# Reordering a decoder layer: the state space branch's input projection ahead of the third attention group, and gate z ahead of the third gate

## The chip, the cores and the metric

The kernel runs on one core of a Trainium2 chip. The metric is the device time of one execution in microseconds (us), the median of three runs. The profile is of one execution more, recorded by the hardware profiler. TensorE (PE in the profile, PEld for its weight loads) multiplies matrices into PSUM; VectorE (DVE), ScalarE (ACT) and GpSimd (POOL) work elementwise; SyncE (SP) issues the DMA transfers.

## The reference

One decoder layer on a sequence of 512 positions of width 1024, all in fp32. A normalised input `u` is projected once, the projection is cut into pieces, and three branches are formed from them, gated and added:

```python
u = rmsnorm(x, ln1_g[i])
proj = u @ w_in[i]
q, k, v, pool_in, z, xbc, dt_raw, gate_pre = jnp.split(proj, split_idx, axis=-1)
y_a = dilated_attention_mixer(q, k, v, rel_bias) @ w_a[i]
y_b = pool_mixer(pool_in, pool_w[i], pool_scale[i]) @ w_b[i]
y_c = ssd_mixer(z, xbc, dt_raw, ...) @ w_c[i]
gates = jax.nn.sigmoid(gate_pre + b_gate[i]).reshape(b, s, N_BRANCH, D_MODEL)
merged = gates[:, :, 0] * y_a + gates[:, :, 1] * y_b + gates[:, :, 2] * y_c
x = x + merged @ w_o[i]
x = x + conv_ffn(rmsnorm(x, ln2_g[i]), ...)
```

- `dilated_attention_mixer`: three groups of six heads (dilations 1, 4, 16), each with its own softmax; their outputs are combined per head by a softmax over the groups' log-sum-exps.
- `ssd_mixer`: a causal convolution of four taps and a Silu on `xbc` (1536 columns: 1024 for x, 256 each for B and C), then a state space scan in four chunks of 128 positions and two groups of eight heads, then a product with `silu(z)`, then a norm over each group's 512 columns.

## The kernel before, in words

**Matmuls.** Every large product is done as three products of split operands (high by high, high by low, low by high; `mm3`, L209). The high part of a weight is a cast on ScalarE (`split`, L176), the low part a subtraction on VectorE (L180).

**Jobs.** The work is a list of `Job`s, one for each weight tile, made by `program()`. Most hold 256 columns of a weight with all 1024 rows (1 MB): two chunks of 128 columns, 24 matmuls of 512 columns each. When job n starts, the main loop's `prepare` splits the weight of job n+1 and fetches those of n+2 and n+3. For n under 34 (`HALVES`) the split is done in two halves, the second at the next step; from 34 on it is done whole, right at the start of the job. `Call` entries between jobs run a function in place.

**Steps and items.** After each chunk (or after two of the four row blocks of a v job, each half of whose 1024 rows is a job) the job calls `step()` (L132). A step advances each generator in the list `running` to its next `yield`, oldest first, then takes the first one from the list `waiting`, starts it and adds it to `running`. So small work is laid between the chunks, and its instructions stand in this order on TensorE, ScalarE, VectorE and GpSimd (`ORDERED`); each of these engines works strictly in that order. SyncE's transfers are ordered by the framework. The items:
- attention (`attend`, `item`): one for each head. For a pair of heads the first item does both score products into two PSUM tiles (L500); each item adds the bias (L514), takes the negative maximum (L518) and does the exponentials with their sums (L521); two steps later it transposes (L527) and copies (L528); the second head of a pair goes on a step later with the product with v (L539). `stats` transposes the maxima and sums (L552, L554).
- `combine`: the weights of the three groups (L570 to L581), a reciprocal (L583), a multiplication on GpSimd (L587), a write to DRAM (L588) and broadcast reads of it into tiles `wb` (L594), with which GpSimd scales the nine output tiles (L596). `split_o` adds and splits them (L602 to L607).
- state space: `xbc_evac` convolves each chunk (L663, L667); `ssd_start` puts the Silus (L827), two transposes and eight `ssd_item`s on the list, with an empty place after each. An `ssd_item` starts with a transpose pxs (L768) and a product pcb (L774), broadcast reads into `al` and `ea`, subtracts and exponentiates (L785, L786), multiplies (L790), and four steps after its start does the products py, pyo and pst (L800, L806, L817), which VectorE adds up (L808, L809, L812, L822).
- `gated` multiplies a chunk by gate z (L853), squares it (L855) and adds the squares (L859): two of the three additions of a group on GpSimd, the last on VectorE. `y_norm` sums over the partitions on TensorE (pss, L867), forms the factor on VectorE and ScalarE (`rstd_of`, L279 to L288, L871), spreads it by TensorE (prb, L875) and scales and splits four tiles (L878 to L885).

**Buffers.** Eight PSUM banks: four tiles tagged "mm" for the chunks, four tagged "sm" for all small products. 52 SBUF tiles of 128x512 (`NBIG`) are shared under one tag.

**The order around the change.** For each attention group: v (two jobs), q and k (three), then `attend` puts its items on the list, so they run beside the next jobs. After the third group come `combine`, the `xbc` projection (six jobs), the first gate (four jobs; the state space items start with its first), then a hand-written row of jobs, `MIX`: g is a job of the third gate, Z and z one of gate z for the first and second half, 0 and 1 put `y_norm` of that half on the list, a is a job of w_a. Before MIX is over what is left on the list is run down by `finish`, then comes w_c.

Of the kernel before, what the change touches and what calls it, by code (L numbers as in the profile page):

```python
# [19 lines left out]
KD = D // P  # L20
# [14 lines left out]
C_XBC = C_Z + D  # L35
# [46 lines left out]
def trunk(ctx: ExitStack, tc, out, x, rel_bias, ln1_g, w_in, b_gate, w_a, pool_w, pool_scale, w_b,  # L82
# [41 lines left out]


    waiting, running = [], []

    second = []

# [4 lines left out]
    def step():  # L134
        flush()
        for it in list(running):
            try:
                next(it)
            except StopIteration:
                running.remove(it)  # L140
        if waiting:
            it = waiting.pop(0)
            running.append(it)
            try:
                next(it)
            except StopIteration:
                running.remove(it)

    def after(n, it):
        for _ in range(n):  # L150
            yield
        yield from it
# [324 lines left out]
    def attend(g):  # L477
        nm = cpool.tile([P, 4, HEADS], F32, name=f"nm{g}")
        ls = cpool.tile([P, 4, HEADS], F32, name=f"ls{g}")
        if g == 0:  # L480
            banks = [[(1, 0, 2), (2, 1, 2)], [(3, 2, 2), (0, 0, 1)]]
        else:
            banks = [[(n, n, 1) for n in range(4)]]
        outs, probs, scores = {}, {}, {}

        def item(h, nb, bank):
            c, hh = h // 2, h % 2
            b = bias_of(g, h)
            off, spans = 0, []
            for n, kb, w in bank:  # L490
                spans.append((n, kb, w, off))
                off += w * P
            if hh == 0:

                q, k = QK["q", g, c], QK["k", g, c]
                pss = [SM("ps"), SM("ps")]
                for n, kb, w, o in spans:
                    for i in range(2):
                        r = slice(DH * i, DH * i + DH)
                        pe.matmul(pss[i][:, o:o + w * P], q[r, n * P:(n + 1) * P],  # L500
                                  k[r, kb * P:(kb + w) * P], start=True, stop=True)
                scores[c, nb] = pss
            ps = scores[c, nb][hh]
            total = off
            sb = T("sb")
            if g == 0 and total == 384:
                dve.tensor_tensor(sb[:, :256], ps[:, :256], b, OP.add)
                dve.tensor_tensor(sb[:, 256:384], ps[:, 256:384], b[:, P:], OP.add)
                for n, kb, w, off in spans:
                    dve.tensor_reduce(nm[:, n, h:h + 1], sb[:, off:off + w * P],  # L510
                                      AX.X, OP.max, negate=True)
            else:
                n = len(bank)
                dve.tensor_tensor(sb.rearrange("p (n c) -> p n c", n=n),  # L514
                                  ps.rearrange("p (n c) -> p n c", n=n),
                                  b.unsqueeze(1).to_broadcast([P, n, S // n]), OP.add)
                n0 = bank[0][0]
                dve.tensor_reduce(nm[:, n0:n0 + n, h], sb.rearrange("p (n c) -> p n c", n=n),  # L518
                                  AX.X, OP.max, negate=True)
            for n, kb, w, off in spans:  # L520
                act.activation(sb[:, off:off + w * P], sb[:, off:off + w * P], AF.Exp,  # L521
                               bias=nm[:, n, h:h + 1], accum_out=ls[:, n, h:h + 1])
            yield
            yield
            pt = SM("pt")
            for o in range(0, total, P):
                pe.transpose(pt[:, o:o + P], sb[:, o:o + P], eye)  # L527
            (act.copy if h % 2 else dve.tensor_copy)(sb[:, :total], pt[:, :total])  # L528
            probs[h, nb] = sb
            if h % 2 == 0:  # L530
                return
            yield
            if c not in outs:
                outs[c] = SM("po")
            po = outs[c]
            for n, kb, w, off in spans:
                for i in range(w):
                    for hh in range(2):
                        pe.matmul(po[DH * hh:DH * hh + DH, n * P:(n + 1) * P],  # L539
                                  V[g, kb + i][:, (2 * c + hh) * DH:(2 * c + hh + 1) * DH],  # L540
                                  probs[2 * c + hh, nb][:, off + i * P:off + (i + 1) * P],
                                  start=i == 0, stop=i == w - 1)
            if nb == len(banks) - 1:
                o = T(f"o{g}")
                act.copy(blocked(o, g), grouped(po, g))
                OT[g, c] = o

        def stats():
            for src, store, nme in ((nm, NM, "nmT"), (ls, LS, "lsT")):
                ps = SM("pst")  # L550
                for n in range(4):
                    pe.transpose(ps[:HEADS, n * P:(n + 1) * P], src[:, n, :], eye)  # L552
                t = T(nme)
                dve.tensor_copy(blocked(t[:HEADS], g), grouped(ps[:HEADS], g))  # L554
                store[g] = t
            return
            yield

        for c in range(3):
            for nb, bank in enumerate(banks):  # L560
                for hh in range(2):
                    waiting.append(item(2 * c + hh, nb, bank))
        waiting.append(after(2, stats()))

    AO = []

    def combine():
        mm, den, tmp = T("mmin"), T("den"), T("dtmp")
        yield
        dve.tensor_tensor(mm[:HEADS], NM[0][:HEADS], NM[1][:HEADS], OP.min)  # L570
        dve.tensor_tensor(mm[:HEADS], mm[:HEADS], NM[2][:HEADS], OP.min)
        for g in range(3):
            n = NM[g][:HEADS]
            dve.tensor_tensor(n, mm[:HEADS], n, OP.subtract)
            act.activation(n, n, AF.Exp)
        yield
        for g in range(3):
            n, l = NM[g][:HEADS], LS[g][:HEADS]
            dve.tensor_tensor(tmp[:HEADS] if g else den[:HEADS], n, l, OP.mult)
            if g:  # L580
                dve.tensor_tensor(den[:HEADS], den[:HEADS], tmp[:HEADS], OP.add)  # L581
        yield
        dve.reciprocal(tmp[:HEADS], den[:HEADS])  # L583
        wd = dram.tile([3, HEADS, S], F32, name="wd")
        for g in range(3):
            n = NM[g][:HEADS]
            pool.tensor_tensor(n, n, tmp[:HEADS], OP.mult)  # L587
            sp.dma_start(wd[g], n)  # L588
        yield
        for c in range(3):  # L590
            for g in range(3):
                wb = T("wb")
                for hh in range(2):
                    sp.dma_start(wb[DH * hh:DH * hh + DH, :],  # L594
                                 wd[g, 2 * c + hh, :].partition_broadcast(DH))
                pool.tensor_tensor(OT[g, c], OT[g, c], wb, OP.mult)  # L596
                if (3 * c + g) % 2:
                    yield

    def split_o(c):  # L600
        for g in (1, 2):
            dve.tensor_tensor(OT[0, c], OT[0, c], OT[g, c], OP.add)  # L602
        ah, al = T("ah", F32R), T("al", F32R)
        act.copy(ah, OT[0, c])
        AO.append((ah, al))
        yield
        dve.tensor_sub(al, OT[0, c], ah.bitcast(F32))  # L607
# [217 lines left out]
    def ssd_start():  # L825
        for m in (8, 9, 0, 1, 2, 3, 10, 4, 5, 6, 7, 11):
            act.activation(XS[m], XS[m], AF.Silu)  # L827
        for gi in range(2):
            waiting.append(btok_item(gi))
        for c, gi, gap in SSD_ORDER:  # L830
            waiting.append(ssd_item(c, gi))
            for _ in range(gap):
                waiting.append(iter(()))
        for c in range(3):
            waiting.append(split_o(c))

    SQ = {0: [], 1: []}

# [250 lines left out]
    def program():  # L1089
# [5 lines left out]
        for g in range(3):  # L1095
# [2 lines left out]
            yield Call(lambda g=g: attend(g))  # L1098
            if g == 0:
                yield Call(lambda: waiting.insert(5, ssd_prep()))  # L1100
        yield Call(lambda: waiting.append(combine()))
        yield from jobs_a(w_in, C_XBC, 12, uhk, ulk, KD, xbc_evac)
        for i, job in enumerate(gate_jobs(0)):
            if i == 0:
                job.body = lambda ws, inner=job.body: (ssd_start(), inner(ws))
            yield job
        many = {"a": branch_jobs(0, w_a, AO, 3), "g": gate_jobs(2),
                "Z": z_jobs(0), "z": z_jobs(1)}
        for token in MIX:
# [185 lines left out]
ORDERED = {EngineType.PE, EngineType.Activation, EngineType.DVE, EngineType.Pool}  # L1295
NBIG = 52
HALVES = 0, 34
MIX = "gggZZ0zzg1aa"
SSD_ORDER = ((0, 0, 1), (1, 0, 1), (0, 1, 1), (2, 0, 1), (1, 1, 1), (3, 0, 1), (2, 1, 1), (3, 1, 1))
WARM = 12  # L1300

# [28 lines left out]
```

## Time and profile before

| | |
|---|---|
| Median of 3 runs | 1066.93 us (1065.83 to 1067.12) |
| Profiled execution | 1067.88 us, of which the span is 1065.7 us |
| Mean granted TensorE clock | 0.994 of full speed |
| DMA | 115.50 MB, mean 108 GB/s |
| GpSimd busy | 13% of the span, in 118 instructions |

The span runs from the first to the last instruction that the profile shows; the rest of the execution's time lies around it. In the profile "L209" is line 209 of the kernel; names such as `pa` or `wl` are tiles; "a<-b,c" is output and inputs; a bracket behind an instruction gives the time for which its engine sat idle before it and what ended that. A line may stand for several instructions in a row (x8).

### The profile page before, as it was taken

What the parts mean: (1) busy time and instruction counts of PE and PEld (TensorE: products, weight loads), DVE (VectorE), ACT (ScalarE), POOL (GpSimd) and SP (SyncE); (2) the same over time, 40 slices, a digit from 0 to 9 for tenths busy, and PEclk for the clock granted to TensorE, in tenths of its full rate; (3) what the DMA queues carried; (4) which work ended last, traced back from release to release, by engine and by line L of the source; (5) the groups of instructions that cost most, each with busy time, mean ns of one, the idle gap of its engine ahead of it and who ended that gap; (6) DMA issues with size and microseconds to landing.
All of it is one profiled execution on the core that took longest, in us unless ns stands there. A gap on an engine that the chain in (4) does not pass through costs nothing.

```text
span 1065.7 us, 12968 instructions
## 1 busy us (share of the span) xinstructions
PE 1047.1 (98%) x5268; PEld 874.1 (82%) x5268; DVE 584.9 (55%) x809; ACT 427.8 (40%) x640; POOL 133.3 (13%) x118
## 2 busy tenths in 40 slices
PE   8999999999999999999999799999999999999997
PEld 8878889888988888877888588898888888888885
DVE  5562433245544668586687856757655565542315
ACT  5342412232435356555544324544444344421312
POOL 1680000000000000621012300001111111110100
PEclk9999999999999999999999899999999999999999
DMA  7235324341542222654322135543232323232312
GB/s 235 77 107 158 109 73 108 98 110 60 143 110 77 81 79 79 178 164 126 90 77 98 54 114 198 163 138 117 83 117 79 117 82 115 83 119 61 117 60 79
DMA packets 116426, 115.50 MB, mean 108 GB/s; under 512 B 5235, under 2 KB 101302, under 8 KB 116367
## 3 DMA queue, kind: packets, MB, share of 16 engines
q1 hardware_dynamic: 116367, 114.68, 35.4%
q8 instruction: 41, 0.67, 0.3%
q14 instruction: 18, 0.15, 0.0%
HBM read 110.87 MB, written 2.22 MB: 106 GB/s over the span
## 4 chain that ended last, share of the span: by engine, by line
PE 93%; DVE 2%; issue 2%; ACT 1%; DMA 1%; POOL 0%; SPq 0%; DVEq 0%; ACTq 0%; POOLq 0%
PE pa L209 33%; PE pu L209 22%; PE pb L209 20%; PE pqk L209 9%; PE ps L500 1%; PE po L539 1%; PE pt L527 1%; PE ppw L209 1%; DVE ytl L885 1%; PE py L800 1%; PE pu L1027 1%; DMA raw<-in_w_in_dram 1%; PE pyo L806 1%; PE pst L817 1%; ACT wh L176 0%
## 5 line engine op out<-in xcount | busy, mean ns | idle before, releaser
L180 DVE TENSOR_TENSOR wl<-raw,wh 128x2048 fp32r<-128x2048 f32 (+4 forms) x126 | 220.8, 1755 | 252.5 <-ACT wh L176 252.4
L176 ACT CAST wh<-raw 128x1024 fp32r<-128x1024 f32 (+4 forms) x128 | 179.4, 1408 | 123.3 <-PE pb L209 76.6
L209 PE MATMUL pa<-uh,wh 128*128 128x512 f32 x384 | 98.3, 398 | 0.3 <-ACT wh L176 0.3
L209 PE MATMUL pa<-ul,wh 128*128 128x512 f32 x384 | 94.9, 389 | 0.0
L994 DVE SCALAR_TENSOR_TENSOR hc<-pu,fcol,hc 128x510 f32<-128x510 f32 x88 | 65.8, 748 | 53.1 <-ACT hc L991 51.5
L209 PE MATMUL pa<-uh,wl 128*128 128x512 f32 x384 | 94.8, 389 | 0.0
L209 PEld LDWEIGHTS pa<-ul,wh 128*128 128x128 f32 x384 | 72.1, 188 | 15.2
L209 PEld LDWEIGHTS pa<-uh,wl 128*128 128x128 f32 x384 | 72.1, 188 | 15.0
L209 PE MATMUL pu<-ul,wh 128*128 128x512 f32 (+1 forms) x352 | 83.5, 379 | 0.0
L209 PE MATMUL pu<-uh,wl 128*128 128x512 f32 (+1 forms) x352 | 83.5, 379 | 0.0
L209 PE MATMUL pu<-uh,wh 128*128 128x512 f32 (+1 forms) x352 | 83.5, 379 | 0.0
L209 PEld LDWEIGHTS pa<-uh,wh 128*128 128x128 f32 x384 | 70.2, 188 | 15.5 <-issue 0.9
L209 PEld LDWEIGHTS pu<-uh,wl 128*128 128x128 f32 x352 | 64.2, 188 | 12.5
L209 PEld LDWEIGHTS pu<-ul,wh 128*128 128x128 f32 x352 | 64.2, 188 | 12.5
L209 PEld LDWEIGHTS pu<-uh,wh 128*128 128x128 f32 x352 | 64.1, 188 | 12.4
L991 ACT ACTIVATE hc<-pu,fcol,fcol 128x512 f32<-128x512 f32 x40 | 31.1, 780 | 81.0 <-PE pu L209 81.0
L999 POOL TENSOR_TENSOR hc<-hc 128x512 f32<-128x512 f32 x22 | 31.5, 1430 | 223.7 <-DVE hc L994 223.6
L521 ACT ACTIVATE sb<-sb,nm 128x128 f32<-128x128 f32 (+1 forms) x72 | 30.1, 419 | 64.4 <-DVE nm L518 49.0
L587 POOL TENSOR_TENSOR nmT<-nmT,dtmp 6x512 f32<-6x512 f32 x3 | 5.6, 1896 | 351.8 <-DVE dtmp L583 351.8
L209 PE MATMUL pb<-wh,fh 128*128 128x512 f32 x176 | 47.7, 389 | 0.0
L209 PE MATMUL pb<-wl,fh 128*128 128x512 f32 x176 | 47.7, 389 | 0.0
L209 PE MATMUL pb<-wh,fl 128*128 128x512 f32 x176 | 47.7, 389 | 0.0
(272 smaller groups left out, 1611.2 us busy)
## 6 DMA issues: line engine op xcount, KB each, us to landing
raw<-in_w_in_dram SPq DMA_DIRECT2D x25, 1024.0 KB
raw<-in_ffn_w_up_dram SPq DMA_DIRECT2D x22, 1024.0 KB
raw<-in_w_in_dram SPq DMA_DIRECT2D x20, 512.0 KB
raw<-in_ffn_w_down_dram SPq DMA_DIRECT2D x10, 1024.0 KB
raw<-in_w_o_dram SPq DMA_DIRECT2D x8, 1024.0 KB
raw<-in_w_in_dram SPq DMA_DIRECT2D x6, 768.0 KB
raw<-in_w_b_dram SPq DMA_DIRECT2D x4, 1024.0 KB
al<-ad SPq DMA_DIRECT2D x16, 256.0 KB
```

Source lines behind the costliest of these rows:

```text
L176: act.copy(h[:, :, o], job.raw[:, :, o])
L180: (eng or dve).tensor_tensor(l[:, :, o], job.raw[:, :, o], h[:, :, o].bitcast(F32), OP.subtract)
L209: pe.matmul(ps, l, r, start=first and n == 0, stop=last and n == total - 1)
L500: pe.matmul(pss[i][:, o:o + w * P], q[r, n * P:(n + 1) * P], k[r, kb * P:(kb + w) * P], start=True, stop=True)
L521: act.activation(sb[:, off:off + w * P], sb[:, off:off + w * P], AF.Exp, bias=nm[:, n, h:h + 1], accum_out=ls[:, n, h:h + 1])
L527: pe.transpose(pt[:, o:o + P], sb[:, o:o + P], eye)
L539: pe.matmul(po[DH * hh:DH * hh + DH, n * P:(n + 1) * P], V[g, kb + i][:, (2 * c + hh) * DH:(2 * c + hh + 1) * DH], probs[2 * c + hh, nb][: ...
L800: pe.matmul(py[DH * i:DH * i + DH, j * P:(j + 1) * P], xc[:, o:o + DH], als[j // 2][:, lo:lo + P], start=True, stop=True)
L806: pe.matmul(po[:, j * P:(j + 1) * P], prev[gi][:, j * P:(j + 1) * P], XS[10 + gi][:, cs], start=True, stop=True)
L991: act.activation(t, ps, AF.Identity, bias=ff["c1"][:, ff["b"] + m:ff["b"] + m + 1], scale=fw(2, m))
L994: dve.scalar_tensor_tensor(t[:, sh:], ps[:, :S - sh], fw(k, m), t[:, sh:], OP.mult, OP.add)
L999: pool.tensor_tensor(a, a, t, OP.mult)
```

## The change: what it does

The xbc projection and `ssd_start` move from behind the third attention group to a place ahead of it, behind the second group's `attend`; so the projection runs beside the second group's items. The empty places that `ssd_start` leaves on the list become a mark, `FREE`, and a new function, `fill`, puts the third group's items into those that are still there, so attention and state space items take turns; what is left over, and then `combine`, goes to the end. In MIX all of gate z and both norms come ahead of the third gate. `combine` loses its first `yield` and takes a whole column of three output tiles at a time, and it starts `split_o` for that column itself.

```diff
     waiting, running = [], []
+    FREE = ()
+
+    def fill(items):
+        for it in items:
+            at = next((i for i, w in enumerate(waiting) if w is FREE), None)
+            if at is None:
+                waiting.append(it)
+            else:
+                waiting[at] = it
...
         if waiting:
-            it = waiting.pop(0)
+            it = iter(waiting.pop(0))
...
-        for c in range(3):
-            for nb, bank in enumerate(banks):
-                for hh in range(2):
-                    waiting.append(item(2 * c + hh, nb, bank))
-        waiting.append(after(2, stats()))
+        fill([item(2 * c + hh, nb, bank) for c in range(3) for nb, bank in enumerate(banks)
+              for hh in range(2)] + [after(2, stats())])
...
         mm, den, tmp = T("mmin"), T("den"), T("dtmp")
-        yield
...
                 pool.tensor_tensor(OT[g, c], OT[g, c], wb, OP.mult)
-                if (3 * c + g) % 2:
-                    yield
+            yield
+            running.append(after(1, split_o(c)))
...
             waiting.append(ssd_item(c, gi))
             for _ in range(gap):
-                waiting.append(iter(()))
-        for c in range(3):
-            waiting.append(split_o(c))
+                waiting.append(FREE)
...
             if g == 0:
                 yield Call(lambda: waiting.insert(5, ssd_prep()))
-        yield Call(lambda: waiting.append(combine()))
-        yield from jobs_a(w_in, C_XBC, 12, uhk, ulk, KD, xbc_evac)
-        for i, job in enumerate(gate_jobs(0)):
-            if i == 0:
-                job.body = lambda ws, inner=job.body: (ssd_start(), inner(ws))
-            yield job
+            if g == 1:
+                yield from jobs_a(w_in, C_XBC, 12, uhk, ulk, KD, xbc_evac)
+                yield Call(ssd_start)
+        yield Call(lambda: fill([after(2, combine())]))
+        yield from gate_jobs(0)
...
-MIX = "gggZZ0zzg1aa"
+MIX = "ZZ0zz1ggggaa"
```

## The prediction

> **What bounds the kernel now.** I read the busy times, then the busy time by stretch, then the order of time where TensorE idles. First the span and the busy shares of the page:
>
> ```profile
> span 1065.7 us, 12968 instructions
> PE 1047.1 (98%) x5268; PEld 874.1 (82%) x5268; DVE 584.9 (55%) x809; ACT 427.8 (40%) x640; POOL 133.3 (13%) x118
> ```
>
> TensorE is the bound: it is idle for only 18.6 us. A reordering that leaves the matmuls as they are can win no more than that and the time lost at a low clock. Four stretches (start:end and length, PE, PEld, DVE, ACT and POOL busy, granted clock, DMA share, GB/s):
>
> ```profile
> 337.00:557.00 220.00, 220.00 (x1194) 177.98 (x1194) 154.64 (x240) 117.53 (x180) 33.90 (x24) 1.00 0.36 106
> 590.00:594.30 4.30, 0.40 (x3) 0.04 (x1) 3.78 (x10) 1.99 (x2) 1.61 (x1) 0.79 0.00 0
> 594.30:599.70 5.40, 5.40 (x12) 3.61 (x13) 4.79 (x5) 1.20 (x2) 2.44 (x2) 0.53 0.35 108
> 606.20:610.30 4.10, 4.05 (x10) 3.00 (x11) 2.97 (x4) 2.42 (x2) 0.00 (x0) 0.59 0.00 0
> ```
>
> Projection, first gate, state space items and gate z (337 to 557) run without a gap on TensorE. The hole comes after them, where the last norm has no projection left to run under. TensorE in order of time:
>
> ```profile
> 589.51 0.84 PE L209 MATMUL pa<-ah,wl 128*128 128x512 f32 x3
> 594.26 2.08 PE L875 MATMUL prb<-dg,ones 128*128 128x512 f32 x2 [3.90 <-DVE dg L871]
> ...
> 606.25 1.45 PE L209 MATMUL pa<-yth,wh 128*128 128x512 f32 x2 [3.00 <-ACT yth L880]
> 607.50 2.97 PE L209 MATMUL pa<-ytl,wh 128*128 128x512 f32 x8
> 610.31 0.85 PE L209 MATMUL pa<-yth,wl 128*128 128x512 f32 x3
> ```
>
> Two waits, 3.90 and 3.00, each with a halved clock behind it.
>
> **What goes: 11.1.** The chain of waits has what this work costs unhindered:
>
> ```profile
> 569.84 0.79 PE pss L867 x8
> 570.62 5.61 PE pa L209 x24
> 576.23 0.92 PE prb L875 x2
> ```
>
> From 590.35 (589.51 + 0.84) to 610.31 are 19.96 us. In them are prb (0.92) and 34 products of 512 columns (18 of the w_a branch, 16 of w_c) at 5.61 / 24 = 0.234, so 7.95: 8.9 in all. The passage loses 11.1 us. After the change eight chunks of the third gate and w_a follow the last gate z, and the last norm runs under them.
>
> **What moves at no cost.** I number steps (one after each 128-column chunk or two row blocks) from the third v projection: v 1-4, q/k 5-10, first gate 11-18, gate z 19-26, third gate 27-34, w_a 35-38. Popping the list by hand: state space items start at 3, 5, ... 17 and reach their products four steps later; attention items take the free places 12, 14, 16, 18, then 19 and 20; the group's statistics come at 23, combine at 24-30; norm 0 has pss at 25 and prb at 26, norm 1 at 29 and 30. The number of matmuls stays. The projection runs beside attention group 2 instead of 3, the same item with the same instructions, hidden by 5.6 us of matmul a step; weight fetches trade places one for one; the scale multiplies on POOL leave the state space stage. Cover is the first stretch above: DVE 154.64 and ACT 117.53 of 220.
>
> **What comes, in the first gate: 7.5.** Tiles tagged "sm" have four PSUM banks. How near that already is, from the chain and from DVE in order of time:
>
> ```profile
> 471.86 1.02 PE py L800 x16
> 472.88 1.09 PE pyo L806 x8
> 473.97 0.86 PE pst L817 x2
> 474.83 0.44 PE pxs L768 x4
> 475.26 0.33 PE pcb L774 x2
> ```
> ```profile
> 472.16 2.29 DVE L180 TENSOR_TENSOR wl<-raw,wh 128x2048 fp32r<-128x2048 f32 x1 [2.50 <-ACT wh L176]
> 474.37 0.68 DVE L808 TENSOR_TENSOR ea<-pyo,ea 128x512 f32<-128x512 f32 x1
> ```
>
> An odd step needs five banks; the fifth (pcb) gets pyo's when L808 has read it, at 475.05. L808 stands behind the weight split's subtraction, that behind the cast on ACT. The change puts an attention item ahead of the cast in each even step. ACT today, the attention item's instructions (min/median/max in ns), and its PE part:
>
> ```profile
> 466.50 0.69 ACT L894 ACTIVATE sg<-pa,col 128x512 f32<-128x512 f32 x1 [2.89 <-issue]
> 467.21 1.28 ACT L786 ACT_TABLE_LOAD   x1
> 468.91 0.63 ACT L786 ACTIVATE al<-al 128x512 f32<-128x512 f32 x1 [0.42 <-DVE al L785]
> 469.69 0.63 ACT L786 ACTIVATE al<-al 128x512 f32<-128x512 f32 x1
> 470.23 1.89 ACT L176 CAST wh<-raw 128x2048 fp32r<-128x2048 f32 x1
> ```
> ```profile
> L521 ACT ACTIVATE sb<-sb,nm x72: 385/388/513, 218.1 to 396.2; 128x128 f32<-128x128 f32 x54, 128x256 f32<-128x256 f32 x18
> L521 ACT ACTIVATION_READ_ACCUMULATOR sb<-sb,nm x72: 185/187/192, 218.5 to 396.5; 128x1 f32 x72
> L514 DVE TENSOR_TENSOR sb<-ps,b x18: 669/682/693, 216.7 to 393.6; 128x512 f32<-128x512 f32 x18
> L518 DVE TENSOR_REDUCE nm<-sb x18: 687/689/690, 217.4 to 394.3; 128x4 f32<-128x512 f32 x12, 128x2 f32<-128x512 f32 x6
> L528 DVE COPY sb<-pt x12: 551/683/691, 227.8 to 399.6; 128x512 f32<-128x512 f32 x9, 128x384 f32<-128x384 f32 x3
> ```
> ```profile
> L785 DVE TENSOR_SCALAR al<-al,acs x64: 269/275/1327, 436.8 to 541.2; 128x128 f32<-128x128 f32 x64
> ```
> ```profile
> 364.38 0.44 PE pt L527 x4
> 364.82 1.09 PE ps L500 x16
> ```
>
> Step 14, from its start on PE: transposes 0.44, copy 0.68 on DVE, eight subtractions of 0.275, add and maximum 1.37 (4.8); four Exp with their accumulators on ACT 2.3 (7.1), cast 1.89 (9.0), subtraction 2.29 (11.3), L808 (12.0). PE: 0.44 + 5.61 + 3.41 for py to pxs = 9.5. So pcb waits 2.5 us. After step 18 the second score tile of the next pair is the fifth: 2.9. After steps 12 and 16 a held score bank makes pxs the one that waits, ACT's chain (sigmoid, table, two Exp, four Exp, cast) being the longer there: 10.4 against 9.7, about 1.0 with the bank after it, twice. Sum 7.4, with semaphores 7.5. Bounds: 1 (DVE early as today, 0.2 a step) and 13 (each subtraction slowed by POOL towards its maximum of 1.33 us).
>
> **At the v projection: 0.8.** Twelve Silu (0.63 each as Exp; a table load 1.28) now stand ahead of the cast for the second v job and of the copies that free banks, 8.8 us; that job's cover is 48 products of 384 columns, an estimate of 8.4 from 0.234, plus small ones. 0 to 2; I take 0.8.
>
> **At the norms: 2.3 and 4.7, and 2.5 of clock.** The softmax combination lands among them. Rows: the norm's first DVE instruction, the reciprocal, and POOL's part:
>
> ```profile
> 592.08 0.15 DVE L279 TENSOR_SCALAR v<-pss 128x4 f32<-128x4 f32 x1
> ```
> ```profile
> 424.77 3.33 DVE L583 RECIPROCAL dtmp<-den 6x512 f32<-6x512 f32 x1
> ```
> ```profile
> 428.27 5.62 POOL L587 TENSOR_TENSOR nmT<-nmT,dtmp 6x512 f32<-6x512 f32 x3 [351.81 <-DVE dtmp L583]
> 440.94 2.53 POOL L596 TENSOR_TENSOR o<-o,wb 128x512 f32<-128x512 f32 x2 [7.04 <-DMA wb<-wd]
> 444.27 1.29 POOL L596 TENSOR_TENSOR o<-o,wb 128x512 f32<-128x512 f32 x1 [0.80 <-issue]
> ```
>
> Norm 0, from step 24 on PE: ACT does Silu 0.69, table 1.28, three Exp 1.9, Square 0.63, cast 1.89 (6.4); DVE subtraction 2.29 (8.7), five passes for the denominator at 0.68 (12.1); then as 592.08 to 594.26, 2.2 to prb (14.3). PE is there at 5.61 + 0.79 + 5.61 = 12.0: 2.3, bounds 0 and 4.
>
> Norm 1: its sum of squares is partly on POOL, in order behind the multiplies by wb, and those behind a DMA round trip. Product with gate z 0.68 (14.9), reciprocal 3.33 (18.2), nmT 5.62 (23.9), wait for wb 7.04 (30.9), three multiplies 3.8 (34.7), the add on POOL 1.3, the last on DVE 0.68: 36.7. PE asks at 14.3 + 0.92 + 3 x 5.61 = 32.0: 4.7, bounds 0 (wb in half the time) and 6.2 (the gap ahead of 444.27 again). Behind the waiting DVE add stand a weight subtraction, needed a job later, and pss itself. After 3.90 idle the 5.40 us at clock 0.53 lost 2.5; I take that once.
>
> Sum: 7.5 + 0.8 + 2.3 + 4.7 + 2.5 = 17.8 against 11.1: **6.7 longer**. The profiled execution took 1067.88 (2.2 around its span), so 1074.6; the median 1066.93 lies 0.95 below it: 1073.6.
>
> **The rivals.**
> - *The engines' slack hides it all*, faster. DVE is 70% and ACT 53% busy in the first stretch. It decides at the odd steps: if the subtraction ends within 2.6 us of py's start, as at 474.45 now, and wb lands some 3 us after nmT, what remains is 1 to 2 us: 1057. Against it: the added 2.3 us stands in ACT's one path to the cast, not in its slack. 0.22.
> - *Half the waits*: 8.9 to 13 come instead of 17.8, within 0.2% (about what a measurement tells from no change). 0.12.
> - *The clock falls at each wait near 3 us.* After 3.00 idle, 4.10 us at 0.59 lost 1.7; at the waits of 2.3, 2.5 and 2.9 that adds 5.1: 1078.7. Against it: that drop came soon after another. 0.18. [...]
> - *Tiles run out.* By my count about 52 of the 52 shared tiles are live in steps 13 to 17 (attention's v, q, k, outputs and statistics beside state space and gates). Another 1 to 2 us in each of five steps: 1081. 0.08.
>
> **How the numbers follow.** The forecast, 1069.1 to 1077, has 0.40. Slower: 0.40 + 0.18 + 0.08 = 0.66; same 0.12; faster 0.22, the slack rival. The likeliest case is the forecast: 1073.6. The range 1058 to 1084 takes in the low bounds (17.8 down to 2.2) and the upper rivals; left out are the clean removal and a worse shortage, 0.15 together.
>
> **What would show it.** Right: no gap between w_a and w_c; pcb, pxs or ps waiting on L808 in the first gate; prb on dg early in gate z's end; pss on the DVE add (L859), itself on POOL, with the clock near 0.5 after it. Wrong: PE busy without a gap from the third v projection to w_c (then 1057), or a subtraction of the split that ends as early after py as now.

## The result, and the profile after

| | before | after |
|---|---|---|
| Median of 5 runs | 1066.93 us (1065.83 to 1067.12) | 1071.57 us (1070.37 to 1072.28) |
| Ratio to before, 95% interval | | 1.0046 (1.0031 to 1.006) |
| Profiled execution, its span | 1067.88, 1065.7 us | 1071.57, 1069.8 us |

The changed kernel is 4.6 us slower; 1073.6 was forecast. Its lines are numbered ten higher around `mm3` (L219), six higher in `combine` and the state space items, and four higher in the norms. The page's first lines:

```profile
span 1069.8 us, 12988 instructions
PE 1047.7 (98%) x5268; PEld 874.4 (82%) x5268; DVE 575.9 (54%) x809; ACT 428.3 (40%) x641; POOL 128.6 (12%) x118
```

TensorE is busy for about as long as before (0.6 us more), so 3.5 of the 4.1 us by which the span is longer are idle time (22.1 us, 18.6 before). Busy time by stretch (start:end, length, PE, PEld, DVE, ACT and POOL busy, granted clock, DMA share, GB/s):

```profile
337.00:557.00 220.00, 213.85 (x1196) 174.06 (x1194) 139.09 (x243) 119.41 (x193) 20.67 (x18) 1.00 0.38 104
549.50:561.70 12.20, 6.05 (x27) 4.69 (x26) 7.59 (x10) 6.07 (x7) 6.93 (x6) 0.86 0.87 231
561.70:569.60 7.90, 7.87 (x25) 6.62 (x26) 7.26 (x8) 0.20 (x1) 6.75 (x4) 0.57 0.43 131
590.00:660.00 70.00, 70.00 (x311) 57.98 (x310) 40.07 (x41) 19.81 (x18) 10.18 (x8) 1.00 0.40 135
```

The last row is where the hole was: w_a and w_c now run without a gap, at full clock. The first row had no gap before; now 6.15 us are idle in it, 3.4 of them at the norms, which now fall into it. TensorE's waits by what ended them (sum, times, longest):

```profile
PE pss L871 <- DVE sq L863: 6.2, 1, 6.2
PE prb L879 <- DVE dg L875: 1.9, 1, 1.9
...
PE ps L510 <- DVE ea L814: 1.2, 1, 1.2
PE pcb L780 <- DVE ea L814: 1.2, 1, 1.2
...
PE pbt L751 <- ACT o L555: 0.3, 1, 0.3
```

The places are those that the prediction named. TensorE after the longest, in order of time:

```profile
561.73 1.83 PE L871 MATMUL pss<-ones,sq 128*128 128x1 f32 x8 [6.18 <-DVE sq L863]
563.42 3.76 PE L219 MATMUL pa<-uh,wh 128*128 128x512 f32 x8
566.98 2.68 PE L219 MATMUL pa<-ul,wh 128*128 128x512 f32 x8
```

Eight products take 3.76 and 2.68 instead of 1.98: the granted clock is 0.57 in the third stretch. Where the time came from, by the start of the same piece of work: the q and k chunk at the end of which the changed order begins starts at 263.39 (264.42 before), the first product of w_o at 653.82 (650.23 before). Between them the kernel lost (653.82 - 650.23) + (264.42 - 263.39) = 4.62 us, which is the whole difference of the medians.

What held pss. GpSimd, then VectorE, then SyncE's issues, in order of time:

```profile
550.23 1.34 POOL L602 TENSOR_TENSOR o<-o,wb 128x512 f32<-128x512 f32 x1 [2.79 <-DMA wb<-wd]
556.11 2.49 POOL L602 TENSOR_TENSOR o<-o,wb 128x512 f32<-128x512 f32 x2 [4.54 <-DMA wb<-wd]
558.54 1.27 POOL L863 TENSOR_TENSOR sq<-sq 128x512 f32<-128x512 f32 x1
559.76 8.69 POOL L602 TENSOR_TENSOR o<-o,wb 128x512 f32<-128x512 f32 x5
```
```profile
559.85 1.73 DVE L863 TENSOR_TENSOR sq<-sq 128x512 f32<-128x512 f32 x1 [4.61 <-POOL sq L863]
561.51 3.35 DVE L190 TENSOR_TENSOR wl<-raw,wh 128x2048 fp32r<-128x2048 f32 x1
...
566.04 1.20 DVE L296 TENSOR_TENSOR rt<-rt,v 128x4 f32<-128x4 f32 x1
...
568.52 0.16 DVE L298 TENSOR_TENSOR r<-rt,r 128x4 f32<-128x4 f32 x1
```
```profile
546.58 1.75 SPq L600 DMA_DIRECT2D wb<-wd  x3
549.85 0.40 SPq L175 DMA_DIRECT2D raw<-in_w_in_dram  x1
550.31 8.90 SPq L600 DMA_DIRECT2D wb<-wd  x13
```

The second addition of squares (558.54) stands behind three multiplies, and these behind the reads of wb. A weight fetch of 1 MB (549.85) is issued between the reads on SyncE: half of the second tile's data is read behind it, GpSimd waited 4.54 us for that tile, and the stretch from 549.50 moved 231 GB/s. That the addition waits behind the multiplies, and these behind a DMA, is the mechanism that was forecast; that the fetch is what made the second tile late is read from the order of the issues, and no run moved it. The VectorE rows show something that was not: its addition took 1.73 where one takes 0.68, its subtraction 3.35 instead of 2.29, and operations on 128x4 elements 1.20, until GpSimd's five multiplies ended at 559.76 + 8.69 = 568.45; the next one, at 568.52, took 0.16.

### The profile page after: what moved, and what is told of

It reads as the page before. It is cut to its first block, busy times and chain, and to the rows that moved or that the text cites. A ratio compares the mean times of both kernels' runs of the same rounds, so it can differ in the third digit from the quotient of the medians.

```text
span 1069.8 us, 12988 instructions
## 1 busy us (share of the span) xinstructions
PE 1047.7 (98%) x5268; PEld 874.4 (82%) x5268; DVE 575.9 (54%) x809; ACT 428.3 (40%) x641; POOL 128.6 (12%) x118
## 4 chain that ended last, share of the span: by engine, by line
PE 88%; DVE 3%; issue 3%; ACT 3%; DMA 1%; POOL 1%; SPq 0%; DVEq 0%; ACTq 0%; POOLq 0%
PE pa L219 31%; PE pu L219 21%; PE pb L219 19%; PE pqk L219 9%; ACT wh L186 1%; PE ps L510 1%; PE pu L1031 1%; PE ppw L219 1%; PE pt L537 1%; PE po L549 1%; DMA raw<-in_w_in_dram 1%; DMA wb<-wd 1%; PE py L806 0%; DVE wl L190 0%; ACT xs L833 0%
## 5 line engine op out<-in xcount | busy, mean ns | idle before, releaser
L219 PE MATMUL pa<-uh,wh 128*128 128x512 f32 x384 | 101.0, 406 | 0.3 <-ACT wh L186 0.3
L219 PE MATMUL pa<-ul,wh 128*128 128x512 f32 x384 | 95.7, 392 | 0.0
L219 PE MATMUL pa<-uh,wl 128*128 128x512 f32 x384 | 94.9, 389 | 0.0
L219 PEld LDWEIGHTS pa<-ul,wh 128*128 128x128 f32 x384 | 72.7, 189 | 15.6
L219 PEld LDWEIGHTS pa<-uh,wh 128*128 128x128 f32 x384 | 71.0, 191 | 16.8 <-issue 1.7
L219 PEld LDWEIGHTS pa<-uh,wl 128*128 128x128 f32 x384 | 72.1, 188 | 15.0
L219 PE MATMUL pu<-uh,wh 128*128 128x512 f32 (+1 forms) x352 | 83.6, 380 | 0.0
L219 PE MATMUL pu<-uh,wl 128*128 128x512 f32 (+1 forms) x352 | 83.5, 379 | 0.0
L219 PE MATMUL pu<-ul,wh 128*128 128x512 f32 (+1 forms) x352 | 83.5, 379 | 0.0
L219 PEld LDWEIGHTS pu<-uh,wl 128*128 128x128 f32 x352 | 64.2, 188 | 12.4
L219 PEld LDWEIGHTS pu<-ul,wh 128*128 128x128 f32 x352 | 64.2, 188 | 12.4
L219 PEld LDWEIGHTS pu<-uh,wh 128*128 128x128 f32 x352 | 64.1, 188 | 12.4
L785 POOL TENSOR_TENSOR xd<-xc,dec 128x512 f32<-128x512 f32 x6 | 6.3, 1044 | 365.7 <-DVE xc L776 365.7
L219 PE MATMUL pb<-wh,fh 128*128 128x512 f32 x176 | 47.7, 389 | 0.0
L219 PE MATMUL pb<-wh,fl 128*128 128x512 f32 x176 | 47.7, 389 | 0.0
L219 PE MATMUL pb<-wl,fh 128*128 128x512 f32 x176 | 47.7, 389 | 0.0
```

The costliest lines, as they stand in the source:

```text
L219: pe.matmul(ps, l, r, start=first and n == 0, stop=last and n == total - 1)
L785: pool.tensor_tensor(h3(xd), h3(xc), hb(dec, c, 8 * gi), OP.mult)
```

## The experiments

Theory at first: four losses of separate causes (PSUM banks, combine in front of norm 0 on VectorE, GpSimd's order in front of norm 1, the clock behind it). Rival: each wait only shows that the small engines are late there, and moves on when it is taken away. Each time stands beside runs of before on the same chip.

### The row of jobs, and the order, each alone

`old_order_new_mix` is the kernel before with the new row of jobs alone; `new_order_old_mix` is the changed kernel with the old row.

```diff
-MIX = "gggZZ0zzg1aa"
+MIX = "ZZ0zz1ggggaa"
```

> The kernel before with the new row of jobs alone (all of gate z and both norms ahead of the third gate); the projection, the third attention group, combine and split_o stay where they were. Theory (the gain is the removed hole of 11.1 us, all losses come from attention and combine landing among state space items and norms): both norms run under the third gate and w_a, combine's GpSimd work is long done, no new wait: 1066.9 - 11 = 1056 to 1058. Rival (gate z right behind the first gate is itself what makes the norms wait, since the state space items end only four chunks later): the waits stay and it is 1065 to 1072.

Measured: 1065.58 against 1066.94, ratio 0.9991 (0.9981 to 1.0). The hole isn't gone; it moved to another wait (on VectorE's multiplication of a chunk of w_a by its gate, which frees the chunk's bank):

```profile
PE pa L209 <- DVE sg L901: 7.2, 1, 7.2
```

Both norms' scaling and w_a's evacuations now meet in w_a's short jobs. The row of jobs alone gives 1.4 us of the 11.1 by the medians, and the interval reaches down to none. That is in the rival's range, though not for its reason: of the norms' own waits only 0.4 at prb is left.

> The changed kernel with the old row of jobs (three jobs of the third gate ahead of gate z, the second norm just ahead of w_a). Theory: the hole ahead of w_c is back (11 us), the waits at the norms (pss, prb) are gone, the PSUM waits in the first gate (3.3 by the trace after) and 0.4 at the v projection stay: 1066.9 + 3.7 = 1070.6, 1069 to 1072. Rival (the losses are those of the norms alone, the PSUM waits are made up again later): 1067.

Measured: 1076.05, ratio 1.0098 (1.0081 to 1.0115), longer than either theory said. Its waits:

```profile
PE pss L871 <- DVE sq L863: 4.1, 1, 4.1
PE prb L879 <- DVE dg L875: 3.3, 1, 3.3
PE pa L219 <- ACT yth L884: 3.2, 2, 3.0
```

The hole at yth is back, and the waits at pss and prb stay, now at norm 0, since combine meets whichever norm runs beside it. So the order is the part that costs (+9.1 alone), and the row pays 4.5 together with it (1076.05 to 1071.57).

### The banks: `pst_in_mm`

```diff
-            pst = SM("pst")
+            pst = MM("pst")
```

The tile of the state goes to the four "mm" banks, so an odd step needs only four of "sm".

> The changed kernel with the state space product pst in one of the four chunk banks instead of a small bank, so that an odd step needs four small banks where it needed five. Theory (the waits of pcb and of the scores in the first gate are for a fifth bank): 3.3 us in the trace after, of which some 2.8 go: 1068.8, 1068 to 1069.5. Rival (the steps are late because VectorE is late, a bank more only moves the wait): 1071 to 1072.

Measured: 1067.26, ratio 1.001 (1.0 to 1.002): 4.3 us less than the changed kernel. No wait at pcb or ps is left in the trace; pss (6.4) and prb (2.0) are as they were. So the fifth bank is the cause of these waits. Set side by side, product by product, the two traces show what it is worth: TensorE of `pst_in_mm` starts the first gate 0.7 us earlier (414.35 against 415.07) and the chunk behind step 19's scores 4.3 us earlier (485.81 against 490.10), so the first gate gains 3.6.

### Norm 1: three tries that fell short

`norm1_a_job_later` asks for norm 1 one job later:

```diff
-MIX = "ZZ0zz1ggggaa"
+MIX = "ZZ0zzg1gggaa"
```

> The changed kernel with the second norm put on the list one job of the third gate later (ZZ0zzg1gggaa); nothing else moves. Theory (pss waits for a GpSimd addition that stands behind the scaling by wb, 6.3 us, and the low clock behind it costs 3.5): pss is asked for two steps, 11 us, later, when the sum is ready: both go, 1071.6 - 9.8 = 1061.8, 1061 to 1063. Rival (VectorE is late there whatever is asked of it, and the wait moves along with the norm): 1068 to 1072.

Measured: 1070.05, ratio 1.0035 (1.0021 to 1.0049). The wait at pss fell from 6.2 to 1.0, and a new one of 3.3 came at prb. The time is the rival's, and the wait did move along; why, `all_mended` shows below.

`sums_on_dve` takes the addition off GpSimd, so that it no longer stands behind the reads of wb:

```diff
-            (dve if len(SQ[gi]) == 4 else pool).tensor_tensor(SQ[gi][0], SQ[gi][0], sq, OP.add)
+            (dve if gi or len(SQ[gi]) == 4 else pool).tensor_tensor(SQ[gi][0], SQ[gi][0], sq, OP.add)
```

> The changed kernel with the second half's additions of squares all on VectorE (two of three were on GpSimd, behind the scaling by wb). Theory (GpSimd's strict order: the addition stands behind multiplications that wait for a DMA, VectorE stands blocked behind it for 4.6 us, and TensorE waits 6.2 for pss): no blocked VectorE, no wait at pss, none moved to prb as when the norm was only asked for later; with the low clock 6.2 + 3.5 go: 1061.8, 1061 to 1063. Rival (VectorE is overloaded by combine and the norm whatever GpSimd does): two more additions of 0.68 make it 1070 to 1073.

Measured: 1069.48, ratio 1.0025 (1.0015 to 1.0035), 2.1 us less than the changed kernel; neither theory's number. pss waits 1.9, prb 3.6 for norm 1. VectorE and GpSimd there, in order of time:

```profile
560.91 0.62 DVE L295 TENSOR_TENSOR rt<-r 128x4 f32<-128x4 f32 x1
...
564.05 1.18 DVE L298 TENSOR_TENSOR r<-rt,r 128x4 f32<-128x4 f32 x1
565.32 1.67 DVE L875 TENSOR_TENSOR dg<-eye,r 128x512 f32<-128x512 f32 x1
```
```profile
558.53 9.58 POOL L602 TENSOR_TENSOR o<-o,wb 128x512 f32<-128x512 f32 x6 [4.89 <-DMA wb<-wd]
```

A chain of five operations (four on 128x4 elements, one on 128x512) takes 6.1 us, from 560.91 to 566.99, while GpSimd multiplies.

`no_wait_for_wb` multiplies each output tile by itself, so that GpSimd waits for no DMA (the combination weights are left out of the output):

```diff
-                pool.tensor_tensor(OT[g, c], OT[g, c], wb, OP.mult)
+                pool.tensor_tensor(OT[g, c], OT[g, c], OT[g, c], OP.mult)
```

> The changed kernel in which GpSimd scales each output tile by itself and not by the broadcast weights, so that the weights of the groups' combination are left out; their DMAs are still issued, nothing waits for them. All engine orders stay. Theory: GpSimd's chain without the round trip ends at 541.95 + 4.24 + 1.29 + 3 x 1.27 + 1.29 = 552.6 in the time of the trace after, ahead of TensorE's 555.4, so the wait goes as with the additions on VectorE: 1061 to 1063. Rival (the order of GpSimd's own 10 us of work is enough, DMA or not): some 1067 to 1070.

Measured: 1074.14, ratio 1.0068 (1.0055 to 1.0082). Taking the DMA wait away brought no gain, against the theory, and a time outside the rival's range. Of the 2.6 us by which it is slower than the changed kernel, its trace puts some 1.6 down to half clock behind norm 0's wait of 1.9 (seven products take 3.19 there and the next eight 2.15, where eight take 1.98 at full clock); the rest is the balance of the waits that this view explains, VectorE, then GpSimd:

```profile
547.97 10.29 DVE L190 TENSOR_TENSOR wl<-raw,wh 128x2048 fp32r<-128x2048 f32 x1 [2.50 <-ACT wh L186]
```
```profile
547.85 3.03 POOL L602 TENSOR_TENSOR o<-o 128x512 f32<-128x512 f32 x3
...
552.08 8.52 POOL L602 TENSOR_TENSOR o<-o 128x512 f32<-128x512 f32 x6
```

The same subtraction takes 2.29 elsewhere. With nothing to wait for, GpSimd's multiplies stand closer together, and VectorE is held for longer: TensorE waited 2.5 for this subtraction and 4.6 at pss. So the second theory: **GpSimd's scaling multiplies hold VectorE up**, and what is late at prb (and part of what is late at pss) is that, not the DMA round trip alone. The expectations below call this theory "port"; by what means the one engine holds the other, no run shows. Rival: VectorE's own queue is too full there.

### Mends together: `both_mended` and `den_on_pool`

`both_mended` has the edits of `pst_in_mm` and `sums_on_dve`.

> The changed kernel with both: pst in a chunk bank and the second half's additions on VectorE. Theory (two separate causes, of 4.3 and 9.8): 1071.6 - 14.1 = 1057.5, 1056.5 to 1059; only prb's 2 us and the v projection's 0.3 stay. Rival (the waits cover for one another): 1061 to 1064.

Measured: 1066.66, ratio 0.9992 (0.9984 to 1.0001). Missed by 9, and above the rival's 1061 to 1064 too: norm 1's wait at prb had grown to 4.2. The gains of the two mends measured alone, 4.3 and 2.1, add up to 1065.2. `den_on_pool` gives GpSimd also the five passes of combine's denominator, which stood in front of norm 0 on VectorE:

```diff
-            dve.tensor_tensor(tmp[:HEADS] if g else den[:HEADS], n, l, OP.mult)
+            pool.tensor_tensor(tmp[:HEADS] if g else den[:HEADS], n, l, OP.mult)
...
-                dve.tensor_tensor(den[:HEADS], den[:HEADS], tmp[:HEADS], OP.add)
+                pool.tensor_tensor(den[:HEADS], den[:HEADS], tmp[:HEADS], OP.add)
```

> As both_mended, and the five passes that form the combination's denominator on GpSimd and not on VectorE, where they stand ahead of the first norm's factor. Theory (prb of norm 0 waits 2 us behind these 3.4 us): a further 2 to 2.5 less than both_mended: 1055.3. Rival (the factor waits for the weight split's cast on ScalarE, and the reciprocal comes later behind the slower GpSimd, so the outputs are late for w_a): no gain, 1057.5 to 1061.

Measured: 1064.04, ratio 0.9969 (0.9958 to 0.998). It is 2.6 below `both_mended`, as expected of the step, though the total is 9 above. Norm 1's wait at prb is 4.5, its small operations at 1.2 as before.

### The "port" theory: `no_scaling_multiplies` and two later norms

`no_scaling_multiplies` is `sums_on_dve` without the nine multiplies; weights are computed, written and read back all the same:

```diff
-                pool.tensor_tensor(OT[g, c], OT[g, c], wb, OP.mult)
```

> As the run that gave 1069.48 (norm 1's sum on VectorE), without GpSimd's nine multiplies by the combination weights; the weights are still computed, written and read back, but the output leaves them out. The norm stands where it stood. Theory (port): with GpSimd idle the small operations between pss and dg take 0.15 to 0.2 us each and dg 0.69, about 4.8 us earlier in all, so norm 1's wait at prb (3.6) is gone and norm 0's 2 us stays; the wait at its sums (1.9) may stay: 1063 to 1066. Rival (VectorE's own queue is late, GpSimd has no part in it): small operations and the wait at prb as they were, 1068 to 1070.

Measured: 1063.2, ratio 0.997 (0.9958 to 0.9982), 6.3 us below `sums_on_dve` (5.9 if each is set against before on its own chip). VectorE in order of time, at the same place (lines one lower):

```profile
560.22 0.16 DVE L295 TENSOR_TENSOR rt<-r 128x4 f32<-128x4 f32 x1
...
561.07 0.69 DVE L874 TENSOR_TENSOR dg<-eye,r 128x512 f32<-128x512 f32 x1
```

The chain takes 1.5 us instead of 6.1; of the waits at prb only norm 0's 1.9 is left. VectorE's own work is the same, so the rival falls. The wait at pss is gone too, but that is no gain: in this execution TensorE ran at half clock behind norm 0's wait (0.50 from 538.57 to 541.98, last section) and ended the products ahead of pss 2.0 us later, so pss starts at the same time as in `sums_on_dve` (556.98 and 556.96).

`sum_dve_norm_later` and `all_mended` are `sums_on_dve` and `den_on_pool` with norm 1 asked for a job later (the edit of `norm1_a_job_later`).

> Norm 1's sum of squares is added on VectorE, as in the run that gave 1069.48, and norm 1 is asked for one job later in the gates' row. Theory (port): in that run norm 1's four small VectorE operations took 0.62 to 1.22 us each instead of 0.16 and dg 1.67 instead of 0.69, because they stood beside GpSimd's six scaling multiplies (558.5 to 568.1). One job later (some 6 us) most of them come after the multiplies, so they take 0.15 to 0.2 us again, the wait for norm 1's sums (1.9) and the 3.6 us for its dg go, with the low clock behind them: 1062 to 1064, and only norm 0's wait of some 2 us is left at prb. Rival (VectorE is late by its own queue, and the wait moves along with the norm, as it did when the norm alone was moved, 1070.05): the wait at prb stays at 3 us or more for norm 1 and the time is 1068 to 1070.

Measured: 1066.97, ratio 1.0004 (0.9994 to 1.0013), between the two.

> The state's PSUM tile in the matmul pool, norm 1's sum of squares on VectorE, the combine's denominator on GpSimd (together 1064.04 before) and norm 1 asked for one job later. Theory (port): norm 1's wait of 4.5 us at prb and most of the 1.9 at its sums go: 1057 to 1060. Rival (the wait moves along with the norm): 1063 to 1065.

Measured: 1062.06, ratio 0.9958 (0.9945 to 0.997), again between. Both have a wait of 3.3 at prb left. A job was not late enough to be clear of GpSimd, as VectorE and GpSimd of `all_mended` show:

```profile
561.01 0.18 DVE L291 RECIPROCAL r<-sq 128x4 f32<-128x4 f32 x1 [2.13 <-ACT sq L290]
561.22 1.24 DVE L295 TENSOR_TENSOR rt<-r 128x4 f32<-128x4 f32 x1
562.50 0.17 DVE L296 TENSOR_TENSOR rt<-rt,v 128x4 f32<-128x4 f32 x1
...
562.90 1.10 DVE L298 TENSOR_TENSOR r<-rt,r 128x4 f32<-128x4 f32 x1
```
```profile
551.97 10.47 POOL L602 TENSOR_TENSOR o<-o,wb 128x512 f32<-128x512 f32 x6 [3.70 <-DMA wb<-wd]
562.72 1.26 POOL L602 TENSOR_TENSOR o<-o,wb 128x512 f32<-128x512 f32 x1 [0.28 <-DMA wb<-wd]
```

GpSimd pauses from 562.44 to 562.72. The two operations that start in or at the edge of that pause take 0.17; those before and after take over a microsecond. Two more delays come with the later place: two of `split_o`'s additions (L608) now stand ahead of the norm's first operation and took 3.46 instead of 1.41, and VectorE waited 2.13 (0.27 in `sums_on_dve`) for the square root, which stands on ScalarE behind `split_o`'s cast and a table load (0.62 and 1.28 in `norm1_a_job_later`, where the wait is 2.18). So in part the wait did move along with the norm, as the rival had it.

### The version that is faster: `scaling_on_dve`

It is `den_on_pool` with the nine multiplies on VectorE, at the head of `split_o`:

```diff
-                pool.tensor_tensor(OT[g, c], OT[g, c], wb, OP.mult)
...
-    def split_o(c):
+    def split_o(c, wbs):
+        for g in range(3):
+            dve.tensor_tensor(OT[g, c], OT[g, c], wbs[g], OP.mult)
```

> As the run that gave 1064.04 (the state's PSUM tile in the matmul pool, norm 1's sum of squares on VectorE, the combine's denominator on GpSimd, the norm where the change put it), with the nine multiplies by the combination weights moved from GpSimd to VectorE, each column's three at the head of the step that adds them; the output is whole. Theory (port): nothing runs on GpSimd beside norm 1's small operations, so they take 0.15 to 0.2 us each and its wait of 4.5 us at prb goes as it did when the multiplies were left out, with about 1.5 us of low clock; VectorE's nine multiplies at 0.68 (6.1 us in three steps) stand behind the norm and hide: 1057 to 1060. Rival (VectorE's own time is what is short there, so 6.1 us more of it come out as a wait elsewhere, at a weight split, a norm multiply or w_a's first operand): 1062 to 1066.

Measured: 1060.01, ratio 0.9941 (0.9928 to 0.9955): the upper edge of what the theory said, 4.0 us below `den_on_pool` (3.5 if each is set against before on its own chip) and 6.7 below before, with the whole output. Norm 1's four small operations take 0.16 to 0.17 us each. Norm 0 and norm 1 together wait 1.3 at pss and prb. Two new waits at the start of w_a, 0.9 and 1.0, come behind VectorE's added 5.7 us:

```profile
PE pa L219 <- ACT wh L186: 1.2, 2, 0.9
...
PE pa L219 <- DVE al L616: 1.0, 1, 1.0
PE pss L874 <- DVE sq L866: 0.8, 1, 0.8
PE prb L882 <- DVE dg L878: 0.5, 1, 0.5
```

## Why the prediction was right, and where its sizes were off

| step | forecast | measured |
|---|---|---|
| hole at w_a and w_c | -11.1 | gone, no gap in 590 to 660 |
| banks in the first gate | 7.5 | 3.6 (`pst_in_mm` against the changed kernel, up to step 19) |
| v projection | 0.8 | 0.3 |
| norm 0 at prb | 2.3 | 1.9 (with the denominator's passes moved away, the time fell by 2.6) |
| norm 1 at pss | 4.7 | 6.2 |
| low clock behind it | 2.5 | 3.4 (9.62 us from 561.73 to 571.35 at 0.65) |
| sum | +6.7 | 15.4 - 11.1 = +4.3 by these, +4.6 by the medians |

**What went.** Right, though with a condition that the forecast did not state: the row of jobs alone only moves the hole (`old_order_new_mix`).

**The banks** are the term that was mis-sized. TensorE, VectorE and ScalarE of the changed kernel at step 15, TensorE also at step 19:

```profile
455.73 0.49 PE L780 MATMUL pcb<-xcv 128*128 128x128 f32 x2 [1.18 <-DVE ea L814]
...
489.01 1.16 PE L510 MATMUL ps<-k,q 64*128 64x128 f32 x14 [1.20 <-DVE ea L814]
```
```profile
452.78 2.29 DVE L190 TENSOR_TENSOR wl<-raw,wh 128x2048 fp32r<-128x2048 f32 x1 [3.51 <-ACT wh L186]
454.99 0.68 DVE L814 TENSOR_TENSOR ea<-pyo,ea 128x512 f32<-128x512 f32 x1
```
```profile
449.31 0.40 ACT L531 ACTIVATE sb<-sb,nm 128x128 f32<-128x128 f32 x1 [0.69 <-DVE nm L528]
449.62 0.19 ACT L531 ACTIVATION_READ_ACCUMULATOR sb<-sb,nm 128x1 f32 x1
449.71 0.39 ACT L531 ACTIVATE sb<-sb,nm 128x128 f32<-128x128 f32 x1
...
450.87 1.88 ACT L186 CAST wh<-raw 128x2048 fp32r<-128x2048 f32 x1
```

The chain is the one worked out: cast, subtraction, L814, and pcb as the fifth bank. But four exponentials with their accumulators take 450.87 - 449.31 = 1.56, not the 2.3 got by adding their durations, since an accumulator's read overlaps the next one (it ends at 449.62 + 0.19 = 449.81, the next exponential starts at 449.71); and they start 449.31 - 445.06 = 4.25 after step 14 does on TensorE, not 4.8. These two make up the 1.3 by which the wait at pcb was forecast too long (2.5 for 1.18). Of the four places forecast, the two behind a held score bank cost little: some 0.5 at step 13, by which pcb is later there than in `pst_in_mm`, and nothing that shows at step 17. Between 414 and 536 the two rows above are the only waits that the view of TensorE marks.

**The norms.** Places and releasers were right. Norm 0 came within 0.4 us. For norm 1 the second wait for wb was not counted (4.54 ahead of 556.11, behind the 1 MB fetch); the sum had one wait of 7.04 and let the multiplies follow it without a pause. The prediction had GpSimd slow VectorE only as an upper bound in the state space items; in the norm, where it decides what a mend is worth, it was left out. In the changed kernel itself it is part of the 6.2 only through the 1.05 that the last addition took too long; the rest of it lies under the products that follow at a low clock.

**The rivals.** *Slack hides it all* (1057) failed as its own point of decision says: the subtraction ended at 452.78 + 2.29 = 455.07, 4.0 after py's start at 451.07, not 2.6. What it would have been worth is near what `scaling_on_dve` reached. *Half the waits* was wrong by a little: 4.6 us are over the 0.2% (2.1 us) that divides them. *The clock falls at waits near 3 us* was not put to the test in this kernel: its waits other than pss were 1.2 to 1.9, and the clock behind the 1.9 was 1.00. That was luck: behind the same wait it was 0.50 in `no_scaling_multiplies`, and in `no_wait_for_wb` seven products took 3.19 (last section). The number of *tiles* shows in no wait of TensorE. Two figures behind the range do not add up: the stated low bounds of the terms come to 1, not 2.2, and the range leaves out the 1057 of a rival with 0.22, but puts only 0.15 outside itself.

## What to carry to other kernels

Work moved to where TensorE never idles meets the order of the small engines there: count, for the first product that needs it, every instruction ahead on ScalarE, VectorE, GpSimd and SyncE, and how many PSUM tiles are live. A wait that is mended one cause at a time only moves while a second cause stands behind it; look for instructions that last longer than their usual duration, not only for idle time. An off-path GpSimd loop beside a chain of small VectorE operations is not free: here it was worth some 4 to 6 us (`scaling_on_dve` is 4.0 below `den_on_pool`, `no_scaling_multiplies` 6.3 below `sums_on_dve`), and doing its nine multiplies on VectorE itself was faster.

## What the runs showed of the hardware

- **VectorE beside GpSimd.** Operations on 128x4 elements that take 0.16 us in `no_scaling_multiplies` took 1.10 to 1.24 beside GpSimd's multiplies (`all_mended`), about one multiply (1.27 us) each. Those that read two tiles were held (L296, 1.20 in the changed kernel), and L297, which reads one, was held as well (1.20 in the changed kernel and 1.22 in `sums_on_dve`, instead of 0.17). The 128x2048 subtraction took 10.29 us in `no_wait_for_wb`, instead of 2.29, beside several of GpSimd's multiplies that stood back to back. That the multiplies cause the delay of the small operations, `no_scaling_multiplies` shows: the chain takes 1.5 us instead of 6.1. By what means they do, no run shows.
- **The granted clock.** Between 45 and 1050 us it is 1.00 or 0.50 in the traces of the kernels before and after. The low stretches last 6.83 and 3.41 us before (592.50 to 599.33 and 606.15 to 609.56) and 10.24 us after (558.20 to 568.44): twice, once and three times 3.41. Two stretches of 3.41 us at norm 0's wait of 1.9 us and behind it, in `sums_on_dve` and then in `no_scaling_multiplies` (start:end and length, PE, PEld, DVE, ACT and POOL busy, granted clock, DMA share, GB/s):

```profile
535.83:539.24 3.41, 1.57 (x5) 1.03 (x6) 3.24 (x8) 1.06 (x2) 0.00 (x0) 1.00 0.28 95
539.24:542.65 3.41, 3.41 (x16) 2.81 (x16) 3.41 (x4) 2.08 (x3) 1.13 (x1) 1.00 0.00 0
```
```profile
535.15:538.57 3.42, 1.48 (x6) 0.78 (x5) 2.94 (x11) 0.21 (x2) 0.00 (x0) 1.00 0.62 215
538.57:541.98 3.41, 3.41 (x8) 2.35 (x7) 3.41 (x2) 2.50 (x3) 0.06 (x1) 0.50 0.00 0
```

With 3.41 - 1.57 = 1.84 us idle in the first of the two, the second kept its clock; with 3.42 - 1.48 = 1.94 it was halved. The same reading of before and after, in stretches of 3.41 us laid from the start of a low one: the stretch behind 1.56 us idle (after, 534.31 to 537.72) was at 1.00; those behind 2.15 and 2.90 idle (before, from 589.08 and from 602.74) and behind 2.65 (after, from 554.79) were at 0.50. Norm 0's wait of 1.94 is cut there, in the changed kernel, into 1.56 and 0.38, and cost no clock. The length of a wait alone does not sort the runs: behind 2.54 in `no_wait_for_wb` eight products took 2.14 us, behind norm 0's 1.9 in the same run seven took 3.19. Nor does the idle time sort them all: in `norm1_a_job_later`, behind a wait of 0.98 at pss, the clock was 0.73 from 562.0 to 566.0 and 0.84 from there to 570.0. What sets it there, no run shows.
